# The down product of a decoder layer: copies in its first block, and the residual rows loaded in pieces in later blocks

## The chip, the cores and the metric

The kernel runs on one core of one Trainium2 chip. The metric is the device time of one execution in microseconds (us), of which the median over several executions counts. A core has five engines that matter here: TensorE (PE in the profile; its weight loads are PEld), VectorE (DVE), ScalarE (ACT), GpSimd (POOL) and SyncE (SP), which issues most of the transfers (DMAs). Each engine works through its own list of instructions in order; semaphores hold an instruction until what it reads is there and what it overwrites is no longer needed. The operands lie in an on-chip memory (SBUF, 128 partitions); PE writes its results to banks of another (PSUM).

## The reference

One layer of a decoder with three token mixers, a merge and an MLP, in float32, on 1024 tokens of width 1024. The change touches the last line only: the residual `x` plus the down product of the MLP, whose inner width is 4096.

```python
x = x + jnp.sum(gate * y, axis=2) @ w_out[layer]

h = rms_norm(x, norm_mlp[layer])
x = x + jnp.square(jax.nn.relu(h @ w_up[layer])) @ w_down[layer]
```

## The kernel before, in words

`tail` computes these lines. It first makes the residual rows `x + ... @ w_out` and stores them to DRAM as `xd`, eight tiles of 128 rows by 1024 columns. Then come the up product and the down product.

*Seven products.* Both matrix products are made by a scheme of Strassen's kind: two by two blocks are multiplied with 7 block products in place of 8, from sums of blocks on each side. The products are named by the numbers 1 to 7. On the weight side of the down product `BSIDE` says which operand each takes: products 1, 2 and 3 take the raw blocks 11, 21 and 22 of `w_down`; 6, 7, 5 and 4 take the sums t2, t3, t1 and t4, which `sums` makes on POOL when they are first asked for (L1266): t1 = 12 - 11, t2 = 22 - t1, t3 = 22 - 12, t4 = 21 - t2. So the operand of product 6 needs three raw blocks and two sums in a row.

*Splits.* Each float32 operand is split into a high and a low part (`split`): ACT copies the source into `wh`, rounded (L90), and DVE or POOL subtracts to get `wl` (L91). The pair is called a form. A product of two forms takes three matmuls (`mm3`, L119 to L121: high by high, high by low, low by high).

*The up product* runs over 16 pairs `p` of weight row blocks. The results of a pair (squares of the relu, L1431 and L1432) are turned into the seven left operands of the down product, each 128 by 512, and stored to DRAM as `ud[p][i]`.

*The down product* is the loop `for b in range(0, H, G)` with H = 16 and G = 2: eight blocks of two pairs each, here called blocks 1 to 8 (block 1 is b = 0). In each block the products come in the order 1, 6, 2, 7, 5, 4, 3. A product takes two forms per pair, one from `ud` (a load by SP at L1523, then a split on ACT and DVE) and one from `w_down` (loads by SP at L1372, sums and splits on POOL, high parts on ACT), four forms in all, and has 24 matmuls of 128 by 512: 4 groups of 128 rows, 2 pairs, 3 matmuls. A block has 168 matmuls. Products 2, 7 and 3 are accumulated into the PSUM banks of 1, 6 and 5.

*What happens to a finished bank.* Products 1, 6 and 7 go to sums `a10` to `a73` in SBUF: in block 1 ACT copies them there (L1540), later DVE adds to them (L1495). Products 2, 5, 4 and 3 belong to one half of an output tile `x1[t]` each, and DVE adds them to it (L1495). In block 1 the eight tiles `x1[t]` are loaded whole from `xd` (L1528) while the forms of products 1 and 6 are made, after the last raw block asked for until then. In block 8 the sums are put together with the tiles and the results are stored.

*Buffers.* Forms: 11, in two pools. Raw blocks `wr`: 3 in the pool `pre` and 4 in `main`. Temporaries by tag: `u` 12, `v` 4, `s` 5 and `e` 4 buffers (`HEAD` = 4). The `s` buffers hold sums of the up weights, the `e` buffers the copy of product 1 in the up product. A buffer is given out anew when the work on its last content is over, so a form of the down product can only be made when an earlier form has been used up by PE.

*Order.* PE's list follows the order of the code. The lists of DVE, ACT, POOL and SP are made when the program is built, by a planner that simulates the engines and puts each instruction where it expects it to be ready; the forms of a product thus move ahead of the matmuls as far as buffers allow, and those of block 1 stand among the last pairs of the up product.

Of the kernel before, what the change touches and what calls it, by code (L numbers as in the profile page):

```python
# [11 lines left out]
F32 = mybir.dt.float32  # L12
F32R = mybir.dt.float32r
AF = mybir.ActivationFunctionType
# [3 lines left out]
P = 128  # L18
S = 1024
D = 1024  # L20
NT = S // P
# [54 lines left out]
class Kernel:  # L76
# [1196 lines left out]
    def tail(self, mp, mh, ml, halves, pre):  # L1273
        tc, nc, a = self.tc, self.nc, self.a
        kw = dict(bufs=1, reuse_waits="tile")
        H = FF // P // 2
        xd = self.dram.tile([NT, P, D], F32, name="xd")
# [7 lines left out]
        for k in range(KT):  # L1285
            r = xp.tile([P, D], F32, name="x1", tag="x1", bufs=2)
# [50 lines left out]
        last = {}  # L1337
        HEAD = 4
        late = []
        for t in (0, 4, 1, 5, 2, 3, 6, 7):  # L1340
            ts = slice(t * P, t * P + P)
            x1 = xp.tile([P, D], F32, name="x1", tag="x1", bufs=2)
            nc.scalar.dma_start(x1, a["x"][ts, :])
            for s in halves:
                ps = self.mm()
# [14 lines left out]
        main = more = None  # L1360
        count = dict(f=0, r=0)
# [3 lines left out]
            pool, bufs = (pre, 3) if main is None or count["f"] % 11 < 3 else (main, 8)  # L1365
            return [pool.tile([P, 512], F32R, name=f"w{x}", tag=f"w{x}", bufs=bufs) for x in "hl"]

        def raw(src):
            count["r"] += 1
            pool, bufs = (pre, 3) if main is None or count["r"] % 7 < 3 else (main, 4)  # L1370
            r = pool.tile([P, 512], F32, name="wr", tag="wr", bufs=bufs)
            last["raw"] = nc.sync.dma_start(r, src).ins  # L1372
            return r

        def temp(tag="u"):
            pool, bufs = dict(u=(more, 12), v=(more, 4), s=(main, 5), e=(main, HEAD))[tag]
            return pool.tile([P, 512], F32, name=tag, tag=tag, bufs=bufs)

        def splitted(src, eng):
            f = form()  # L1380
            self.split(*f, src, eng)
            return f
# [4 lines left out]
        def up_pair(p):  # L1387
            o = Pair()
            wu = lambda n: raw(a["wu"][p + H * (n[0] == "2"), :, (int(n[1]) - 1) * 512:int(n[1]) * 512])
            get = self.sums(wu, lambda: temp("s"), "s", nc.vector)  # L1390
            o.ps, o.p4 = {}, None
# [63 lines left out]
        main = tc.alloc_tile_pool(name="main", side="right", **kw)  # L1455
# [35 lines left out]
        x1 = [acc.tile([P, D], F32, name=f"x1{t}") for t in range(NT)]  # L1491
# [3 lines left out]
        add = lambda o, x: nc.vector.tensor_tensor(o, o, x, op=ALU.add)  # L1495
        G = 2
        order = (1, 6, 2, 7, 5, 4, 3)
        banks = 0

        def bank():  # L1500
            nonlocal banks
            banks += 1
            return self.mm() if (banks - 1) % 8 < 6 else self.tr()

        for b in range(0, H, G):
            gets = []
            for p in range(b, b + G):
                wd = lambda n, p=p: raw(a["wd"][p + H * (n[0] == "2"), :, (int(n[1]) - 1) * 512:int(n[1]) * 512])
                gets.append(self.sums(wd, temp, "t", nc.gpsimd))
            held = {}  # L1510
            final = b + G == H
            if final:
                for j in range(4):
                    add(sums[6][j], sums[1][j])
                    add(x1[j][:, hi], sums[6][j])
                    add(sums[7][j], sums[1][j])
                    add(x1[4 + j][:, lo], sums[7][j])
                    add(x1[4 + j][:, hi], sums[7][j])
            for i in order:
                forms = []  # L1520
                for q in range(G):
                    u = temp("u" if b else "v")
                    nc.sync.dma_start(u, ud[b + q][i])  # L1523
                    forms.append((splitted(u, nc.vector), splitted(gets[q](self.BSIDE[i]), nc.gpsimd)))
                if b == 0 and i in (1, 6):
                    with tc.issue_after(last["raw"]):
                        for t in range(4 * (i == 6), 4 + 4 * (i == 6)):
                            nc.sync.dma_start(x1[t], xd[t])  # L1528
                chain = {2: 1, 7: 6, 3: 5}.get(i)
                if not chain:  # L1530
                    held[i] = [bank() for _ in range(4)]
                for j in range(4):
                    ps = held[chain or i][j]
                    js = slice(j * P, j * P + P)
                    for q in range(G):
                        (uh, ul), (wh, wl) = forms[q]
                        self.mm3(ps, uh[:, js], ul[:, js], wh, wl, q == 0 and not chain, q == G - 1, bool(chain))
                    if i in sums and not final:
                        if b == 0:
                            nc.scalar.activation(sums[i][j], ps, AF.Copy)  # L1540
                        else:
                            add(sums[i][j], ps)
                        continue

                    t, s = place[i](j)
                    for t, s in {1: ((j, hi), (4 + j, lo), (4 + j, hi)), 6: ((j, hi),),
                                 7: ((4 + j, lo), (4 + j, hi))}.get(i, ((t, s),)):
                        add(x1[t][:, s], ps)
                    if final and i in (2, 3, 4, 5):
                        nc.sync.dma_start(a["out"][t * P:(t + 1) * P, s], x1[t][:, s])  # L1550
# [62 lines left out]
```

## Time and profile before

| | us |
|---|---|
| three runs | 2003.59, 2010.27, 2010.7 |
| their median | 2010.27 |
| the profiled execution | 2011.07 |
| its span, first to last instruction | 2009.3 |
| what lies around the span | 1.77 |

The profile shows one execution. The mean clock that TensorE was granted in it is 0.983 of full speed. The down product begins at 1673.5 us of the span and ends with it.

A row of the timeline has the start, the duration, the engine, the line, the operation, the tile written and the tiles read, the shapes and how many instructions the row joins; in square brackets stands how long the engine was idle ahead of it and what it waited for. A row of a window has, for each engine, its busy time with the number of instructions, then TensorE's granted clock, the busy share of the DMA engines and what they moved. A row of a group has the busy time, the mean duration in ns of one instruction, and the idle time ahead of them with its releaser.

### The profile page before, as it was taken

The numbers are of one execution on the slowest core, as the hardware profiler recorded it, in microseconds if no ns is written. First come the engines' busy times: TensorE is split into PE (matmuls) and PEld (weight loads), VectorE is DVE, ScalarE is ACT, GpSimd is POOL, SyncE is SP. The second block draws the span as 40 slices with busy tenths as digits, with TensorE's granted clock in tenths as the row PEclk, the third lists the DMA queues.
The fourth block names the chain that finished last, engine by engine and source line by source line (L and its number), as shares of the span: only waits on it lengthen the run. The fifth ranks groups of instructions, "written<-read, shape, count | busy, mean of one in ns | idle before, by whom it ended". The sixth has DMA issues, their size and how long they took to land. (4 is left out here: it accounts for less than half of the span.)

```text
span 2009.3 us, 30615 instructions
## 1 busy us (share of the span) xinstructions
PE 1889.3 (94%) x9842; PEld 1616.0 (80%) x9842; DVE 1422.2 (71%) x3216; ACT 1006.1 (50%) x2550; POOL 959.3 (48%) x1138
## 2 busy tenths in 40 slices
PE   7999999998899999999999899998999998999998
PEld 6788889887788888887888677886788886888876
DVE  6757777788667677658777847648754544889898
ACT  5356555666545555545556524225554454433431
POOL 4455445643361112262232247218454545789784
PEclk9999999999999999999999899999999998999999
DMA  6131012101201111203333366425544436445343
GB/s 222 52 106 56 9 57 54 53 16 55 83 32 57 52 52 59 78 27 101 95 123 125 127 236 208 141 85 177 192 155 146 163 136 236 142 157 163 121 147 115
DMA packets 123773, 221.59 MB, mean 110 GB/s; under 512 B 14580, under 2 KB 35604, under 8 KB 123612
## 3 DMA queue, kind: packets, MB, share of 16 engines
q1 hardware_dynamic: 122028, 213.87, 32.4%
q10 hardware_dynamic: 1584, 5.77, 0.9%
q8 instruction: 78, 1.28, 0.3%
q14 instruction: 83, 0.68, 0.1%
HBM read 158.68 MB, written 64.83 MB: 111 GB/s over the span
## 5 line engine op out<-in xcount | busy, mean ns | idle before, releaser
L91 POOL TENSOR_TENSOR wl<-wr,wh 128x512 fp32r<-128x512 f32 (+3 forms) x246 | 328.5, 1342 | 261.3 <-ACT wh L90 212.6
L90 ACT ACTIVATE wh<-wr 128x512 fp32r<-128x512 f32 (+3 forms) x258 | 150.0, 590 | 189.1 <-PE mm L120 117.2
L716 PE MATMUL sc<-st 128*128 128x256 f32 (+5 forms) x736 | 183.6, 344 | 18.3 <-ACT p L748 17.7
L90 ACT ACTIVATE ph<-tr 128x384 fp32r<-128x384 f32 (+3 forms) x280 | 138.4, 497 | 118.3 <-PE tr L764 96.3
L91 DVE TENSOR_TENSOR pl<-tr,ph 128x384 fp32r<-128x384 f32 (+3 forms) x280 | 155.5, 558 | 40.1 <-ACT ph L90 38.3
L761 POOL MEMSET ph<- 128x128 f32 x152 | 33.9, 223 | 267.8 <-PE ac L904 238.3
L119 PE MATMUL mm<-hh,wh 128*128 128x512 f32 x384 | 159.8, 416 | 0.0
L716 PEld LDWEIGHTS sc<-st 128*128 128x128 f32 x736 | 123.5, 193 | 38.5 <-ACT p L748 29.5
L120 PE MATMUL mm<-hl,wh 128*128 128x512 f32 x384 | 152.4, 397 | 0.0
L121 PE MATMUL mm<-hh,wl 128*128 128x512 f32 x384 | 152.3, 397 | 0.0
L119 PE MATMUL mm<-wh 128*128 128x512 f32 x352 | 140.0, 398 | 8.4 <-DVE x L1495 5.4
L120 PE MATMUL mm<-wl,wh 128*128 128x512 f32 x352 | 139.4, 396 | 9.0 <-POOL wl L91 9.0
L90 ACT ACTIVATE wh<-u 128x512 fp32r<-128x512 f32 x162 | 93.1, 620 | 105.9 <-PE mm L120 27.8
L121 PE MATMUL mm<-wh,wl 128*128 128x512 f32 x352 | 139.0, 395 | 0.0
L764 PE MATMUL tr<-ident,p 128*128 128x128 f32 x792 | 129.8, 277 | 8.5 <-DVE st L569 7.0
L748 ACT ACTIVATE p<-sc,mc 128x256 f32<-128x256 f32 (+5 forms) x200 | 106.7, 539 | 50.8 <-DVE mc L740 47.5
L904 PE MATMUL ac<-ph,st 128*128 128x256 f32 x392 | 110.2, 299 | 18.3 <-DVE ob L911 12.3
L91 POOL TENSOR_TENSOR wl<-s,wh 128x512 fp32r<-128x512 f32 x64 | 89.2, 1401 | 77.9 <-ACT wh L90 77.9
L91 DVE TENSOR_TENSOR wl<-u,wh 128x512 fp32r<-128x512 f32 x98 | 113.6, 1160 | 4.7 <-ACT wh L90 4.7
L119 PE MATMUL mm<-wh,hh 128*128 128x384 f32 (+1 forms) x320 | 115.9, 362 | 0.6 <-ACT raw L525 0.6
L905 PE MATMUL ac<-pl,st 128*128 128x256 f32 x392 | 106.2, 291 | 7.6 <-DVE pl L91 7.0
L120 PE MATMUL mm<-wl,hh 128*128 128x384 f32 (+1 forms) x320 | 109.2, 341 | 0.0
(312 smaller groups left out, 5726.7 us busy)
## 6 DMA issues: line engine op xcount, KB each, us to landing
ud<-u SPq DMA_DIRECT2D x112, 256.0 KB, 2.1
u<-ud SPq DMA_DIRECT2D x98, 256.0 KB, 3.5
wr<-wu SPq DMA_DIRECT2D x76, 256.0 KB, 2.8
wr<-wd SPq DMA_DIRECT2D x64, 256.0 KB, 3.0
gd<-go SPq DMA_DIRECT2D x48, 256.0 KB, 2.0
g<-gd SPq DMA_DIRECT2D x48, 256.0 KB, 3.2
wr<-wg SPq DMA_DIRECT2D x40, 256.0 KB, 2.6
wr<-wbr SPq DMA_DIRECT2D x40, 256.0 KB, 3.0
```

What stands on the lines that cost most here:

```text
L90: nc.scalar.activation(hi, src, AF.Copy)
L91: (eng or nc.vector).tensor_tensor(lo, src, hi.bitcast(F32), op=ALU.subtract)
L119: mm(out, lh, rh, start=first, stop=False, skip_group_check=more)
L120: mm(out, lh, rl, start=False, stop=False, skip_group_check=more)
L121: mm(out, ll, rh, start=False, stop=last, skip_group_check=more)
L716: self.nc.tensor.matmul(ps[:, off:off + k1 - k0], q[:, t * P:(t + 1) * P], k[:, k0:k1], start=i == 0, stop=i == 1)
L748: self.last_exp = self.nc.scalar.activation(p, ps, AF.Exp, bias=m, scale=-1.0, accum_out=l).ins
L761: nc.gpsimd.memset(ph[0:rows, o:o + P].bitcast(F32), 0.0)
L764: nc.tensor.transpose(pt[0:rows, o:o + P], src, self.ident)
L904: nc.tensor.matmul(ac, v, ph, start=first, stop=False)
L905: nc.tensor.matmul(ac, v, pl, start=False, stop=last)
```

## The change

The diff touches `tail` alone.

```diff
--- before.py
+++ after.py
@@ -1365,10 +1365,13 @@
             pool, bufs = (pre, 3) if main is None or count["f"] % 11 < 3 else (main, 8)
             return [pool.tile([P, 512], F32R, name=f"w{x}", tag=f"w{x}", bufs=bufs) for x in "hl"]
 
-        def raw(src):
-            count["r"] += 1
-            pool, bufs = (pre, 3) if main is None or count["r"] % 7 < 3 else (main, 4)
-            r = pool.tile([P, 512], F32, name="wr", tag="wr", bufs=bufs)
+        def raw(src, spare=False):
+            if spare:
+                r = main.tile([P, 512], F32, name="wr", tag="e", bufs=HEAD)
+            else:
+                count["r"] += 1
+                pool, bufs = (pre, 3) if main is None or count["r"] % 7 < 3 else (main, 4)
+                r = pool.tile([P, 512], F32, name="wr", tag="wr", bufs=bufs)
             last["raw"] = nc.sync.dma_start(r, src).ins
             return r
 
@@ -1495,6 +1498,8 @@
         add = lambda o, x: nc.vector.tensor_tensor(o, o, x, op=ALU.add)
         G = 2
         order = (1, 6, 2, 7, 5, 4, 3)
+        rest = [(t, s) for t in range(NT) for s in halves]
+        count["x"] = 0
         banks = 0
 
         def bank():
@@ -1505,8 +1510,9 @@
         for b in range(0, H, G):
             gets = []
             for p in range(b, b + G):
-                wd = lambda n, p=p: raw(a["wd"][p + H * (n[0] == "2"), :, (int(n[1]) - 1) * 512:int(n[1]) * 512])
-                gets.append(self.sums(wd, temp, "t", nc.gpsimd))
+                wd = lambda n, p=p: raw(a["wd"][p + H * (n[0] == "2"), :, (int(n[1]) - 1) * 512:int(n[1]) * 512], p == 1)
+                early = iter("ss" if b == 0 else "")
+                gets.append(self.sums(wd, lambda early=early: temp(next(early, "u")), "t", nc.gpsimd))
             held = {}
             final = b + G == H
             if final:
@@ -1522,10 +1528,12 @@
                     u = temp("u" if b else "v")
                     nc.sync.dma_start(u, ud[b + q][i])
                     forms.append((splitted(u, nc.vector), splitted(gets[q](self.BSIDE[i]), nc.gpsimd)))
-                if b == 0 and i in (1, 6):
-                    with tc.issue_after(last["raw"]):
-                        for t in range(4 * (i == 6), 4 + 4 * (i == 6)):
-                            nc.sync.dma_start(x1[t], xd[t])
+                if b and rest and count["x"] % 2 == 0:
+                    t, s = rest.pop(0)
+                    r = main.tile([P, 512], F32, name="xr", tag="e", bufs=HEAD)
+                    nc.sync.dma_start(r, xd[t][:, s])
+                    add(x1[t][:, s], r)
+                count["x"] += 1
                 chain = {2: 1, 7: 6, 3: 5}.get(i)
                 if not chain:
                     held[i] = [bank() for _ in range(4)]
@@ -1543,6 +1551,9 @@
                         continue
 
                     t, s = place[i](j)
+                    if b == 0:
+                        nc.scalar.activation(x1[t][:, s], ps, AF.Copy)
+                        continue
                     for t, s in {1: ((j, hi), (4 + j, lo), (4 + j, hi)), 6: ((j, hi),),
                                  7: ((4 + j, lo), (4 + j, hi))}.get(i, ((t, s),)):
                         add(x1[t][:, s], ps)
```

In block 1 nothing is loaded into `x1[t]` any more: products 2, 5, 4 and 3 of that block are copied there by ACT, as products 1, 6 and 7 are copied to their sums. The residual comes later: from block 2 on, at every second product, as long as any of 16 pieces is left, a piece of `xd` (128 rows by 512 columns) is loaded into a buffer of the tag `e`, as `xr`, and added to its half of `x1[t]` by DVE with both inputs in SBUF.

The second part concerns buffers in block 1. Its first two sums of each pair, t1 and t2, are made in buffers of the tag `s` instead of `u`. The raw blocks of its second pair (p = 1) go to buffers of the tag `e` and no longer count in the rotation of the `wr` buffers.

The planner's lists move as follows. Lines behind the change have other numbers in the changed program: L1495 becomes L1498, L1540 becomes L1548, L1431 and L1432 become L1434 and L1435.

**POOL, from the end of the up product into block 1.** Before: `wr_18918` and `wr_18930` are block 11 of the two pairs, 18978 and 18996 block 22, 18980 and 18998 block 12, 19050 and 19062 block 21. The sums into `u_18982` and `u_18984` are t1 and t2 of the first pair, `u_19000` and `u_19002` those of the second.

```order
L91 TENSOR_TENSOR wl_18921<-wr_18918,wh_18920 128x512
L91 TENSOR_TENSOR wl_18933<-wr_18930,wh_18932 128x512
L91 TENSOR_TENSOR wl_19053<-wr_19050,wh_19052 128x512
L1266 TENSOR_TENSOR u_18982<-wr_18980,wr_18918 128x512
L1266 TENSOR_TENSOR u_18984<-wr_18978,u_18982 128x512
L1266 TENSOR_TENSOR u_19000<-wr_18998,wr_18930 128x512
L91 TENSOR_TENSOR wl_18987<-u_18984,wh_18986 128x512
L1266 TENSOR_TENSOR u_19002<-wr_18996,u_19000 128x512
L1266 TENSOR_TENSOR u_19102<-wr_18978,wr_18980 128x512
L1266 TENSOR_TENSOR u_19114<-wr_18996,wr_18998 128x512
L1266 TENSOR_TENSOR u_19206<-wr_19050,u_18984 128x512
L91 TENSOR_TENSOR wl_19005<-u_19002,wh_19004 128x512
```

After: 18974 and 18992 are block 22, 18976 and 18994 block 12. The row of `s_18980` is t2 of the first pair (its t1 stands three rows ahead of it); the `wl` rows from 18767 to 18853 are splits of the last up pair.

```order
L1266 TENSOR_TENSOR s_18980<-wr_18974,s_18978 128x512
L91 TENSOR_TENSOR wl_18767<-s_18743,wh_18766 128x512
L91 TENSOR_TENSOR wl_18786<-wr_18783,wh_18785 128x512
L91 TENSOR_TENSOR wl_18807<-s_18804,wh_18806 128x512
L91 TENSOR_TENSOR wl_18830<-wr_18741,wh_18829 128x512
L91 TENSOR_TENSOR wl_18853<-s_18850,wh_18852 128x512
L91 TENSOR_TENSOR wl_18921<-wr_18918,wh_18920 128x512
L91 TENSOR_TENSOR wl_18933<-wr_18930,wh_18932 128x512
L91 TENSOR_TENSOR wl_18983<-s_18980,wh_18982 128x512
L1266 TENSOR_TENSOR s_18996<-wr_18994,wr_18930 128x512
L1266 TENSOR_TENSOR s_18998<-wr_18992,s_18996 128x512
L91 TENSOR_TENSOR wl_19001<-s_18998,wh_19000 128x512
```

Both sums of the first pair now stand ahead of five splits of the last up pair, and those of the second pair directly behind the split of the first pair's t2. The split of block 21 of the first pair (`wl_19053` before, `wl_19045` after), an operand of product 2, stood ahead of all these sums and now stands behind them, and the t3 and t4 sums (`u_19102`, `u_19114`, `u_19206` before) no longer stand between the two t2 splits.

**ACT at the same place.** Before, the copies of product 1 into `a10` to `a13` stand ahead of the high parts of both t2 operands, `wh_18986` and `wh_19004`.

```order
L1431 ACTIVATE u_18869<-u_18764 128x512
L1540 ACTIVATE a10_18900<-mm_18940 128x512
L1432 ACTIVATE u_18869<-u_18869 128x512
L1540 ACTIVATE a11_18901<-mm_18941 128x512
L1540 ACTIVATE a12_18902<-mm_18942 128x512
L1540 ACTIVATE a13_18903<-mm_18943 128x512
L90 ACTIVATE wh_18986<-u_18984 128x512
L90 ACTIVATE wh_18992<-v_18990 128x512
L90 ACTIVATE wh_19004<-u_19002 128x512
```

After, these high parts are `wh_18982` and `wh_19000`; `u_18801` is a result of the last up pair.

```order
L90 ACTIVATE wh_18932<-wr_18930 128x512
L90 ACTIVATE wh_18970<-v_18968 128x512
L90 ACTIVATE wh_18982<-s_18980 128x512
L90 ACTIVATE wh_18988<-v_18986 128x512
L1434 ACTIVATE u_18801<-mm_18724 128x512
L1435 ACTIVATE u_18801<-u_18801 128x512
L90 ACTIVATE wh_19000<-s_18998 128x512
L90 ACTIVATE wh_19038<-v_19036 128x512
```

Both now stand among the last up pair's work, and the first copy of product 1 follows eight rows behind `wh_19038`.

**DVE in block 2, product 2.** `x10` to `x13` are output tiles, `mm_` banks of PSUM, the `wl_` rows splits of `u` operands. Before:

```order
L91 TENSOR_TENSOR wl_19535<-u_19532,wh_19534 128x512
L1495 TENSOR_TENSOR x10_18892<-x10_18892,mm_19328 128x512
L91 TENSOR_TENSOR wl_19545<-u_19542,wh_19544 128x512
L1495 TENSOR_TENSOR x11_18893<-x11_18893,mm_19329 128x512
L1495 TENSOR_TENSOR x12_18894<-x12_18894,mm_19330 128x512
L1495 TENSOR_TENSOR x13_18895<-x13_18895,mm_19331 128x512
L91 TENSOR_TENSOR wl_19587<-u_19584,wh_19586 128x512
L1495 TENSOR_TENSOR a70_18908<-a70_18908,mm_19396 128x512
L91 TENSOR_TENSOR wl_19599<-u_19596,wh_19598 128x512
```

After, with the pieces `xr_19606` and `xr_19840`:

```order
L91 TENSOR_TENSOR wl_19533<-u_19530,wh_19532 128x512
L1498 TENSOR_TENSOR x10_18892<-x10_18892,mm_19320 128x512
L91 TENSOR_TENSOR wl_19543<-u_19540,wh_19542 128x512
L1498 TENSOR_TENSOR x11_18893<-x11_18893,mm_19321 128x512
L1498 TENSOR_TENSOR x11_18893<-x11_18893,xr_19606 128x512
L1498 TENSOR_TENSOR x12_18894<-x12_18894,mm_19322 128x512
L1498 TENSOR_TENSOR x12_18894<-x12_18894,xr_19840 128x512
L1498 TENSOR_TENSOR x13_18895<-x13_18895,mm_19323 128x512
L91 TENSOR_TENSOR wl_19585<-u_19582,wh_19584 128x512
L1498 TENSOR_TENSOR a70_18908<-a70_18908,mm_19391 128x512
L91 TENSOR_TENSOR wl_19597<-u_19594,wh_19596 128x512
```

The list is the same but for two adds of pieces among those from PSUM. All sixteen stand in this way among adds from PSUM and splits: two at the end of block 1, then 4, 3, 4 and 3 in blocks 2 to 5, the two shown among them. From block 6 on DVE's list differs in one exchanged pair of rows.

On SP the loads of whole `x1[t]` tiles stood among the last stores of `ud`, seven of them between the stores of products 2 and 5 of the last pair, ahead of five loads of `w_down`. After, the first `xr` load stands between the stores of products 1 and 4 of the last pair, and the others are spread among the loads of `u` and `w_down` of the blocks that follow.

## Prediction

> **What bounds the kernel now.** I read the span and the engines' shares first, then cut the down product into stretches.
>
> ```profile
> span 2009.3 us, 30615 instructions
> PE 1889.3 (94%) x9842; PEld 1616.0 (80%) x9842; DVE 1422.2 (71%) x3216; ACT 1006.1 (50%) x2550; POOL 959.3 (48%) x1138
> core 0: us, PE busy (x) PEld busy (x) DVE busy (x) ACT busy (x) POOL busy (x), PEclk, DMA share, GB/s
> 1673.50:1678.90 5.40, 5.40 (x25) 4.32 (x23) 4.95 (x5) 3.58 (x6) 3.57 (x3) 1.00 0.88 309
> 1678.90:1694.10 15.20, 8.12 (x20) 5.42 (x20) 3.85 (x5) 5.53 (x10) 10.91 (x9) 0.66 1.03 390
> 1700.00:1912.00 212.00, 211.37 (x932) 174.71 (x931) 181.84 (x228) 87.71 (x159) 176.65 (x120) 1.00 0.44 143
> 1912.00:1982.20 70.20, 60.53 (x245) 46.63 (x243) 68.36 (x84) 22.82 (x41) 54.64 (x35) 0.95 0.37 118
> 1982.20:2006.30 24.10, 23.40 (x102) 19.05 (x102) 21.62 (x33) 5.02 (x9) 7.88 (x5) 1.00 0.43 160
> ```
>
> TensorE (PE) bounds the program, and the down product has three regimes. From 1700 to 1912 PE is busy for 211.4 of 212 us. From 1912 to 1982 VectorE (DVE) is, 68.4 of 70.2 us, and PE does only 245 matmuls. And in 1678.9 to 1694.1, inside block 1, nothing is full but the DMA engines: PE is busy for 8.1 of 15.2 us. That hole is what the change can reach. PE's rows in it:
>
> ```profile
> 1673.50 0.39 PE L119 MATMUL mm<-wh 128*128 128x512 f32 x1
> 1678.71 0.39 PE L121 MATMUL mm<-wh,wl 128*128 128x512 f32 x1
> 1680.31 0.50 PE L119 MATMUL mm<-wh 128*128 128x512 f32 x1 [1.20 <-ACT wh L90]
> 1681.65 0.50 PE L120 MATMUL mm<-wl,wh 128*128 128x512 f32 x1 [0.84 <-POOL wl L91]
> 1683.99 0.79 PE L119 MATMUL mm<-wh 128*128 128x512 f32 x1 [1.60 <-ACT wh L90]
> 1688.21 0.79 PE L120 MATMUL mm<-wl,wh 128*128 128x512 f32 x1 [3.43 <-POOL wl L91]
> 1688.81 0.63 PE L121 MATMUL mm<-wh,wl 128*128 128x512 f32 x1
> 1693.50 0.53 PE L120 MATMUL tr<-wl,wh 128*128 128x512 f32 x1
> 1693.87 0.39 PE L121 MATMUL tr<-wh,wl 128*128 128x512 f32 x1
> ```
>
> Product 1 of block 1 has 24 matmuls, started in 1673.50 to 1678.71: 5.21/23 = 0.2265 us each, 5.44 per product, 38.05 per block. Product 6 should begin at 1678.94. Full pace returns with the start at 1693.87, 14.93 us later, and 17 matmuls were done by then (five from 1680.31 to 1688.21, twelve from 1688.81 to 1693.50), which need 17 x 0.2265 = 3.85. **The hole costs 14.93 - 3.85 = 11.08 us.** Of it 2.4 is clock: the last twelve came 4.69/11 = 0.426 apart, 0.20 too slow.
>
> ```profile
> 1682.00:1684.00 2.00, 0.40 (x3) 0.01 (x1) 0.15 (x1) 0.63 (x1) 2.00 (x2) 0.89 1.03 334
> 1684.00:1686.00 2.00, 0.78 (x1) 0.27 (x1) 0.00 (x0) 0.00 (x0) 2.00 (x3) 0.50 0.95 337
> ```
>
> The granted clock fell to 0.50 after gaps of 1.4, 1.1 and 1.8 us with single matmuls between them. The Trainium skill, "TensorE: Matmul & The Clock Gate", section "Part 1: The HAM clock gate", says half clock follows an idle window of about 3.4 us, free-running; by it gaps like these need not lower the clock, and the hole would be 8.7; here they did, so the measured 11.08 stands.
>
> What ends last in the hole is on POOL and ScalarE (ACT):
>
> ```profile
> 1671.51 1.30 POOL L91 TENSOR_TENSOR wl<-wr,wh 128x512 fp32r<-128x512 f32 x1 [15.01 <-ACT wh L90]
> 1672.77 1.30 POOL L1266 TENSOR_TENSOR u<-wr 128x512 f32<-128x512 f32 x1
> 1681.56 1.71 POOL L1266 TENSOR_TENSOR u<-wr,u 128x512 f32<-128x512 f32 x1
> 1683.24 2.48 POOL L1266 TENSOR_TENSOR u<-wr 128x512 f32<-128x512 f32 x2
> 1685.68 1.25 POOL L1266 TENSOR_TENSOR u<-wr,u 128x512 f32<-128x512 f32 x1
> 1686.90 1.25 POOL L91 TENSOR_TENSOR wl<-u,wh 128x512 fp32r<-128x512 f32 x1
> 1679.14 0.60 ACT L1540 ACTIVATE a<-mm 128x512 f32<-128x512 f32 x1 [0.76 <-PE mm L121]
> 1679.63 0.62 ACT L90 ACTIVATE wh<-u 128x512 fp32r<-128x512 f32 x1
> 1683.30 0.63 ACT L90 ACTIVATE wh<-u 128x512 fp32r<-128x512 f32 x1 [2.53 <-POOL u L1266]
> ```
>
> POOL stood 15 us before a split meant for product 2, so the sums for product 6 began only at 1672.77; the first `wh` of it then waited on ACT behind four copies of product 1 (the last at 1679.14), and the second half's `wl` (1686.90) behind three sums that nobody needed yet. It is an order, and the saturated DMA is not its cause.
>
> **The change, part by part.**
>
> *Earlier sums and reordering (gain 11.08).* The changed program makes `t1`, `t2` of pair 0 among the forms of the last up pair, where POOL has 1.3 us splits 2.7 us apart or more, and those of pair 1 right after the split of pair 0's `t2`; no split of product 2 stands before any of them now. On ACT both `wh` stand ahead of the first copy. I date them by the old rows: the form buffers come free with the up products (5.44/2 = 2.72 us each, the last ending at 1673.5), so pair 0's `t2` can be split near 1660, pair 1's by about 1669, ten microseconds before 1678.94. New sum rows on POOL are 1.3 each and lie in its idle 15 us. What is late next would be the product 2 split of pair 1: its buffer frees with product 1 near 1678.3, it takes ACT 0.62 and POOL 1.3 to 1.75, and it is needed after 1684.4. So I take the whole 11.08; the bounds are 9.7 (the 1.4 us gap stays) and 11.08.
>
> *Residual loads moved.* Eight loads of 512 KB, 8.3 us each to landing, leave block 1; 16 of 256 KB come in blocks 2 to 5, the same 4 MB over 152 us: 27 GB/s on top of 143, no bound. SP issues them in its one order: 16 issues against 8, 0.38 us each as in the row below, and from the fifth on each waits for a buffer that an earlier add frees.
>
> ```profile
> 1761.61 0.38 SPq L1523 DMA_DIRECT2D u<-ud  x1
> ```
>
> *Sixteen adds of block 1 become ACT copies.* The DVE add from PSUM was 0.679; the ACT copy is 0.60 and ACT is busy for 87.7 of 212 us. Hidden under PE; DVE has 10.9 us less in block 1.
>
> *Sixteen adds come to DVE, 2 at the end of block 1, 4, 3, 4 and 3 in blocks 2 to 5.* Both inputs lie in SBUF, and before has no such add beside a PE at full pace. The nearest rows:
>
> ```profile
> L91 DVE TENSOR_TENSOR wl<-u,wh 128x512 fp32r<-128x512 f32 x73 | 85.9, 1178 | 2.4 <-ACT wh L90 2.4
> L91 DVE TENSOR_TENSOR wl<-v,wh 128x512 fp32r<-128x512 f32 x4 | 5.9, 1503 | 1.8 <-ACT wh L90 1.8
> L1495 DVE TENSOR_TENSOR x<-x,mm 128x512 f32<-128x512 f32 x79 | 53.3, 679 | 11.7 <-PE mm L121 11.2
> L1495 DVE TENSOR_TENSOR x<-x,a x12: 678/918/1801, 1949.8 to 1973.0; 128x512 f32<-128x512 f32 x12
> 1658.65 0.68 DVE L91 TENSOR_TENSOR wl<-v,wh 128x512 fp32r<-128x512 f32 x1
> x<-xd SPq DMA_DIRECT2D x8, 512.0 KB, 8.3
> ```
>
> An add costs from 0.68 (POOL idle, as in the row at 1658.65) to 1.80; I take 1.18, the mean of the 73 splits that also read two SBUF tiles in that very stretch. DVE idles 212 - 181.84 = 30.2 us there, 5.4 per block and 21.7 in blocks 2 to 5. Fourteen adds take 16.5 (9.5 to 25.2). At 1.18 they fit, also in a block with four (4.7 of 5.4). Cover of a late add: its PSUM bank is wanted soonest after product 3, 0.75 product or 4.1 us later. At 1.80 they overrun by 3.5 us, to which a half-clock stretch of 2.4 may come: 5.9. Cost taken: 0.
>
> *The end.* From 1912 DVE holds PE, as its 68.4 of 70.2 us show. From block 6 on its order is the same but for one swapped pair, so the 24 + 70 us move as a whole, if DVE comes there without a backlog; block 6 has no added add and 5.4 us of idle to clear one.
>
> **Sum.** The profiled run took 2011.07 (2009.3 span and 1.77 around it). 2011.07 - 11.08 + 0 = **2000.0**. That execution is 0.8 over the median 2010.27 and near the highest of the three (2003.59 to 2010.7); I don't correct for it. About 0.5% is what a measurement of this kernel can tell from no change: 2000.2 from the median, which happens to lie on my number.
>
> **Rivals.**
>
> *DVE and POOL crowd each other in blocks 2 to 5.* For it: splits cost 1.18 instead of 0.68 beside POOL. Against: 21.7 us of idle. Price 5.9 at the upper bound: 2005.9. Were the two never at work at the same time, POOL's 120 instructions at the lone 1.30 and DVE's 73 + 4 splits at 0.68 would hold 208.4 of the 212 us already, and 2.6 of the free 3.6 would fall to blocks 2 to 5; fourteen adds more, 9.5 us, overrun that by 6.9: 2006.9. The Trainium skill, "SBUF — State Buffer", section "Who interferes with whom", states this: a DVE instruction with two SBUF inputs and a GpSimd one that reads SBUF exclude each other for the whole instruction; the trace agrees in kind (0.68 alone, 1.18 beside POOL).
>
> *The hole shrinks but stays.* A gap of 1.4 at 1678.94 remains: 2001.4; with a half-clock stretch 2003.8. For it: the lists on ACT and POOL are long and in order. Against: ten microseconds of lead.
>
> *The end gains too.* POOL's order in the last block differs:
>
> ```profile
> 1959.63 0.50 PE L120 MATMUL mm<-wl,wh 128*128 128x512 f32 x1 [2.76 <-POOL wl L91]
> ```
>
> If this 2.76 goes and DVE profits: 1997.2. Against: DVE was busy all through it.
>
> *Slower than before: SP's queue.* A residual load waits for a DVE add, and behind it stand the `u` and `wd` loads of the next products. From issue to a form a load needs 0.38 + 3.5 + 0.62 + 1.18 = 5.7 us. Eleven form buffers at four a product let the splits run 1.75 products, 9.5 us, ahead of PE. If DVE lags by over 9.5 - 5.7 = 3.8 us the loads come late, PE stops as in the hole, and DVE lags more. Two such holes: 2000.0 + 22.2 = 2022. Against: a lag of that size is cleared within a block by the 5.4 us of idle, and a wait for SP stops none of the work that already lies loaded.
>
> ```profile
> u<-ud SPq DMA_DIRECT2D x98, 256.0 KB, 3.5
> ```
>
> That the residual isn't moved out of block 1 is excluded: the changed order has no load of it before the last up stores and no PSUM add in block 1.
>
> **How the numbers follow.** Forecast 2000.0 (1998 to 2002): 0.52. DVE and POOL crowd: 0.20. Hole stays in part: 0.12. The end gains: 0.12. SP's queue: 0.04. The range for 8 in 10 reaches from 1995.5 (1997.2 less half a microsecond of spread and 1.2 for a clock stretch in the end saved) to 2007.5 (2006.9 and half a microsecond of spread); SP's queue is left out. Faster by over 0.5% is under 2000.2: 0.36 of the forecast's 0.52, as the median lies 0.8 under the profiled run, and the end's 0.12: 0.48. Within 0.5%: 0.16 + 0.20 + 0.12 = 0.48. Slower: 0.04.
>
> **What would show it.** PE's rows around 1679 run on at 0.23 us with the granted clock at 1.00, and POOL's two `t2` sums lie before that. DMA share in block 1 falls from 1.03 to under 0.7. In blocks 2 to 5 DVE is busy for over 93%, the new adds have a mean near 1.2, and PE has no gap over 0.5 us; a gap there with DVE or POOL as releaser speaks for the first rival, one with a DMA as releaser for SP's queue. From block 7 on DVE is full as before, with PE's last 102 matmuls unbroken. The forecast is wrong if a stall outside 1679 to 1694 changes by over 2 us.

## The result, and the profile after

| | before | after |
|---|---|---|
| median of six runs (us) | 2009.19 | 1996.87 |
| lowest and highest | 2003.59, 2014.93 | 1993.05, 2003.03 |
| profiled execution | 2011.07 | 1996.93 |
| its span | 2009.3 | 1995.1 |

The ratio of after to before is 0.9948, 95% interval 0.9933 to 0.9963: faster by 0.5%, 10.4 us, between 7.4 and 13.5. The two medians alone lie 12.3 us apart, within that interval.

First the totals of the changed kernel, with the same columns as before.

```profile
span 1995.1 us, 30648 instructions
PE 1883.6 (94%) x9842; PEld 1612.9 (81%) x9842; DVE 1432.7 (72%) x3216; ACT 1013.8 (51%) x2566; POOL 966.1 (48%) x1138
```

The down product has 1344 matmuls, 168 to a block, and the trace of each kernel has them all, so the stretches can be cut exactly where a block starts: block 1, blocks 2 to 6, blocks 7 and 8. The windows of before:

```profile
1673.50:1722.67 49.17, 42.09 (x169) 33.39 (x168) 31.25 (x34) 23.92 (x44) 37.69 (x27) 0.90 0.69 247
1722.67:1914.04 191.37, 190.74 (x841) 157.63 (x840) 164.32 (x208) 77.17 (x140) 161.30 (x109) 1.00 0.45 148
1914.04:2005.44 91.40, 81.73 (x337) 63.99 (x335) 88.82 (x115) 26.78 (x49) 60.47 (x39) 0.96 0.37 123
```

and of after:

```profile
1670.18:1708.26 38.08, 38.08 (x170) 31.53 (x168) 27.97 (x20) 29.64 (x56) 32.66 (x21) 1.00 0.58 197
1708.26:1900.73 192.47, 191.00 (x841) 157.53 (x840) 178.15 (x223) 77.59 (x142) 165.48 (x109) 1.00 0.50 163
1900.73:1991.39 90.66, 82.78 (x337) 65.40 (x335) 86.48 (x112) 26.77 (x48) 60.86 (x39) 0.92 0.37 123
```

Block 1 became **11.09 us** shorter and PE is now busy in all of it. Blocks 2 to 6 became 1.10 longer, blocks 7 and 8 0.74 shorter. That is 10.73 us less for the down product (331.94 before, 321.21 after, with the last matmul). The span is some 14 us shorter; of the rest 3.32 lies ahead of the down product, which began at 1673.50 before and at 1670.18 after, and some 0.1 behind it.

The first two rows, of PE's timeline, are the end of product 1 and the start of product 6 in block 1; POOL's and ACT's rows show when the operands of product 6 were made. Again from the profile of the changed kernel:

```profile
1675.39 0.39 PE L121 MATMUL mm<-wh,wl 128*128 128x512 f32 x1
1675.62 0.39 PE L119 MATMUL mm<-wh 128*128 128x512 f32 x1
1656.29 1.29 POOL L91 TENSOR_TENSOR wl<-s,wh 128x512 fp32r<-128x512 f32 x1 [0.16 <-ACT wh L90]
1661.43 1.29 POOL L1266 TENSOR_TENSOR s<-wr 128x512 f32<-128x512 f32 x1 [3.86 <-DMA wr<-wd]
1662.80 1.29 POOL L1266 TENSOR_TENSOR s<-wr,s 128x512 f32<-128x512 f32 x1
1664.83 1.29 POOL L91 TENSOR_TENSOR wl<-s,wh 128x512 fp32r<-128x512 f32 x1 [0.74 <-ACT wh L90]
1664.12 0.63 ACT L90 ACTIVATE wh<-s 128x512 fp32r<-128x512 f32 x1 [1.68 <-POOL s L1266]
1671.74 0.60 ACT L1548 ACTIVATE a<-mm 128x512 f32<-128x512 f32 x1
```

Product 6 follows product 1 by 0.23 us. Its two t2 splits (the rows that read `s`) began at 1656.29 and 1664.83, 19.3 and 10.8 us ahead of it, and ACT made the second high part 7.6 us before its first copy of product 1.

### The profile page after: what moved, and what is told of

Its sections match the earlier page's. It is cut to its first block, busy times and chain, and to the rows that moved or that the text cites. A ratio compares the mean times of both kernels' runs of the same rounds, so it can differ in the third digit from the quotient of the medians.

```text
span 1995.1 us, 30648 instructions
## 1 busy us (share of the span) xinstructions
PE 1883.6 (94%) x9842; PEld 1612.9 (81%) x9842; DVE 1432.7 (72%) x3216; ACT 1013.8 (51%) x2566; POOL 966.1 (48%) x1138
## 5 line engine op out<-in xcount | busy, mean ns | idle before, releaser
L91 POOL TENSOR_TENSOR wl<-wr,wh 128x512 fp32r<-128x512 f32 (+3 forms) x246 | 329.2, 1344 | 255.8 <-ACT wh L90 208.6
L91 POOL TENSOR_TENSOR wl<-s,wh 128x512 fp32r<-128x512 f32 x68 | 95.1, 1406 | 78.6 <-ACT wh L90 78.5
L904 PE MATMUL ac<-ph,st 128*128 128x256 f32 x392 | 110.2, 299 | 17.8 <-DVE ob L911 11.9
```

The lines of the kernel that those rows point to most:

```text
L91: (eng or nc.vector).tensor_tensor(lo, src, hi.bitcast(F32), op=ALU.subtract)
L904: nc.tensor.matmul(ac, v, ph, start=first, stop=False)
```

## The experiments

All kernels below are cut in the same way. The numbers are us from the first to the last matmul of each stretch; the down product's start is that of its first matmul in the span.

```
kernel                        start    block 1  2 to 6   7 and 8  span
before                        1673.50  49.17    191.37   91.40    2009.3
after                         1670.18  38.08    192.47   90.66    1995.1
after, once more              1670.29  38.08    192.54   90.58    1995.2
sums part alone               1672.79  38.08    191.57   90.55    1996.7
residual part alone           1666.46  50.46    192.74   91.81    2006.4
tag s alone                   1664.49  38.08    191.54   92.33    1990.2
spare raw buffers alone       1669.76  50.70    191.54   90.53    2006.3
tag s, first pair             1671.25  45.48    191.46   93.37    2005.4
tag s, second pair            1672.08  45.36    191.54   91.84    2004.6
after, no pieces              1667.35  38.08    191.55   90.84    1991.6
after, pieces added twice     1664.16  38.08    196.75   92.13    1994.9
sums, block 8 folded, POOL    1670.00  38.08    191.57   92.77    1996.3
sums, folded, POOL last       1667.06  38.08    191.30   85.86    1989.3
sums, folded, DVE only        1668.04  38.08    191.54   89.27    1991.6
```

### The changed kernel once more

No edit.

> The changed kernel once more, for the spread of one profile: block 1 38.1, blocks 2 to 6 within 0.5 us of 192.5, blocks 7 and 8 within 0.5 us of 90.7; the start of the down product may move by several us, as it lay between 1664.5 and 1673.5 us in six kernels whose program ahead of the last up pairs is the same.

It took 1997.02 us. The blocks came out within 0.08 us of the first profile. In this one repeat the stages of a kernel thus come out within a tenth of a us, and differences of 0.9 us between kernels can be read there. What does not repeat between kernels is the start of the down product: it lies between 1664.16 and 1673.50 in the fourteen profiles, and before happens to be the latest of all. This spread is there long before the change can act: PE's 8001st matmul starts between 1550.39 and 1560.62 us, again latest before, while the lists of PE, DVE, ACT and POOL are the same in all fourteen up to some 50 us ahead of the down product.

### One part of the change at a time

The sums part alone: the pieces' loop goes out, the loads of whole tiles and the adds of block 1 come back.

```diff
-                if b and rest and count["x"] % 2 == 0:
...
-                    add(x1[t][:, s], r)
-                count["x"] += 1
+                if b == 0 and i in (1, 6):
+                    with tc.issue_after(last["raw"]):
+                        for t in range(4 * (i == 6), 4 + 4 * (i == 6)):
+                            nc.sync.dma_start(x1[t], xd[t])
...
-                    if b == 0:
-                        nc.scalar.activation(x1[t][:, s], ps, AF.Copy)
-                        continue
```

> The changed kernel with its early sums and spare raw buffers alone: the whole x1 tiles are loaded in block 1 and added to there by DVE, as before. Order theory: the hole of block 1 comes from POOL's and ACT's order, so block 1 takes 38.1 us as in the changed kernel (49.2 before) although DMA is as full as before; the time is that of the changed kernel or some 2 us less, as the sixteen adds of pieces are gone. DMA theory (the 4 MB of residual loads in block 1 made the operands late): block 1 takes 44 us or more.

The residual part alone: the changed kernel with these two lines.

```diff
-                ..., p == 1)
-                early = iter("ss" if b == 0 else "")
+                ...)
+                early = iter("")
```

> The changed kernel with its residual part alone (copies in block 1, pieces loaded and added in later blocks); sums t1 and t2 of block 1 and all raw blocks in the buffers of before. POOL's order puts both t2 sums behind the splits of the up product again. Order theory: block 1 takes 45 to 49 us, and the time is that of before within 5 us. DMA theory: block 1 takes 40 us or less and the time is near the changed kernel's.

The sums part alone ran in 1998.49 us (median of 4), ratio to before 0.9947 (0.9930 to 0.9965): the whole gain. The residual part alone ran in 2010.66 (10 runs), ratio 1.0004 (0.9989 to 1.0020): none of it. Windows over the first two products of block 1, at full pace 10.9 us long; the columns are those of the other windows, the last two the DMA share and GB/s. Before, then the sums part alone, then the residual part alone:

```profile
1673.50:1695.47 21.97, 14.89 (x49) 10.86 (x48) 9.24 (x9) 10.29 (x19) 15.86 (x12) 0.77 1.00 369
```

```profile
1672.79:1683.66 10.87, 10.87 (x49) 9.01 (x48) 9.42 (x8) 8.36 (x16) 10.24 (x7) 1.00 0.98 356
```

```profile
1666.46:1689.72 23.26, 14.06 (x49) 10.26 (x48) 9.95 (x9) 10.27 (x19) 18.52 (x14) 0.78 0.66 215
```

With the whole tiles still being loaded and the DMA engines 0.98 full, PE runs without a gap; with the DMA share down to 0.66 the hole is as wide as ever. The DMA theory falls, the order theory stands. Block 1 of the residual part alone took 50.46 us, a little above the 45 to 49 expected and 1.3 above before: PE's last wait for POOL in the hole is 5.55 us there and was 3.43.

### Which part of the sums part

The kernel with the sums part alone, without the spare raw buffers, and then without the tag s:

```diff
-                ..., p == 1)
+                ...)
```

> As the kernel with the sums part alone, but the raw blocks of the second pair of block 1 stay in the rotation of before; only t1 and t2 go to the tag s. POOL's order has the sums of the first pair early and those of the second pair where they can be ready a few rows later. If the tag s alone does it: block 1 within 1 us of 38.1. If the spare raw buffers are needed too, for block 12 and 22 of the second pair: 40 to 46 us.

```diff
-                early = iter("ss" if b == 0 else "")
+                early = iter("")
```

> As the kernel with the sums part alone, but t1 and t2 stay in the tag u; only the raw blocks of the second pair go to the tag e. POOL's order keeps the sums behind the last splits of the up product. Order theory: block 1 takes 45 to 49 us as before, since the u buffers and not the raw blocks held the sums back. If the raw blocks were what came late: 38 to 41 us.

They took 1992.07 and 2008.06 us (one run each). Block 1 is 38.08 with the tag s alone, and 50.70 with the spare raw buffers alone. POOL's rows of the latter show that the raw blocks were not what came late:

```profile
1667.77 1.30 POOL L91 TENSOR_TENSOR wl<-wr,wh 128x512 fp32r<-128x512 f32 x1 [11.03 <-ACT wh L90]
1669.02 1.31 POOL L1266 TENSOR_TENSOR u<-wr 128x512 f32<-128x512 f32 x1
```

POOL stands 11 us before a split as it stood 15 before the change, and the first sum follows right behind, with no wait of its own. (The 50.70 is above the 45 to 49 expected, for the same longer wait for POOL, 5.83 us.) What the spare buffers do is elsewhere: blocks 7 and 8 take 90.53 with them and 91.40 without (before); 90.55 with them and 92.33 without where the tag s is in.

The kernel with the tag s alone, narrowed to one pair, so that it differs from the kernel before in two sums:

```diff
-                early = iter("ss" if b == 0 else "")
+                early = iter("ss" if p == 0 else "")
```

> The kernel before with one edit: t1 and t2 of the first pair of block 1 go to the tag s, those of the second pair stay in u. If both pairs are needed (the hole is two stalls, the second one for the second pair's low part): the first stall goes, the second stays in part, block 1 takes 41 to 46 us, its first low-part wait shows on POOL. If the first pair alone made the hole: within 1 us of 38.1.

and with `p == 1`:

> The kernel before with one edit: t1 and t2 of the second pair go to the tag s, those of the first pair stay in u. The first pair's operand is needed first and its sums stay behind the last splits of the up product, so the first stall stays; block 1 takes 41 to 46 us. If the hole is one queue that only has to be shortened by two sums anywhere, 39 us or less.

They took 2007.10 and 2006.37 us (one run each); block 1 is 45.48 and 45.36, so either pair alone leaves two thirds of the hole (7.4 and 7.3 of 11.1 us). PE's longest waits in it, with the rows of POOL behind the longer one, for the first pair early and then for the second pair early:

```profile
1678.05 0.50 PE L119 MATMUL mm<-wh 128*128 128x512 f32 x1 [0.53 <-ACT wh L90]
1682.28 0.79 PE L120 MATMUL mm<-wl,wh 128*128 128x512 f32 x1 [3.72 <-POOL wl L91]
1673.14 3.44 POOL L1266 TENSOR_TENSOR u<-wr 128x512 f32<-128x512 f32 x2
1680.51 1.71 POOL L91 TENSOR_TENSOR wl<-u,wh 128x512 fp32r<-128x512 f32 x1
```

```profile
1678.89 0.49 PE L119 MATMUL mm<-wh 128*128 128x512 f32 x1 [1.21 <-ACT wh L90]
1683.10 0.79 PE L120 MATMUL mm<-wl,wh 128*128 128x512 f32 x1 [3.71 <-POOL wl L91]
1673.98 3.44 POOL L1266 TENSOR_TENSOR u<-wr 128x512 f32<-128x512 f32 x2
1681.34 1.71 POOL L91 TENSOR_TENSOR wl<-u,wh 128x512 fp32r<-128x512 f32 x1
```

It is the same wait for whichever pair's sums are late, behind the same queue on POOL: the late pair's t2 is done by 1673.2 and 1674.0, and its split stands behind the sums t3 and t4 of both pairs, which products 7 and 4 want later. Only with both pairs early is the queue no longer in the way. These waits are 4.3 and 4.9 us of the two holes; most of the rest is clock, as the matmuls right behind them start 0.4 us apart and more, where 0.23 is full pace.

### The price of the pieces

The changed kernel without the pieces, and with every piece added twice:

```diff
-                if b and rest and count["x"] % 2 == 0:
...
-                count["x"] += 1
```

> The changed kernel without loads and adds of the pieces (so the residual is left out). If the pieces are what delays POOL's split by 1.5 us ahead of block 5, blocks 2 to 6 take 190.4 to 191 us (192.5 in the changed kernel, 190.4 is PE's own pace). If POOL's order alone does it, the delay stays as in the kernel with the sums part alone: 191.6. Block 1 as in the changed kernel, 38.1.

```diff
                     add(x1[t][:, s], r)
+                    add(x1[t][:, s], r)
```

> The changed kernel with every piece of the residual added twice (so the residual counts double). Theory of idle time: an add of 1.1 us goes into DVE's idle time until that is used up; blocks 2 to 5 have about 11 us of it left in the changed kernel and get 14 adds more, 15.6 us, so blocks 2 to 6 take 194 to 198 us (192.5 with single adds). Theory of exclusion (DVE with two SBUF inputs and POOL never at work together): POOL and DVE are full at the single adds already and each further add costs its 1.1 us in full: 205 us or more. If the pieces are free: below 193.

They took 1993.65 and 1996.93 us (one run each). Blocks 2 to 6 are 191.55, 192.47 and 196.75 with none, single and double adds. So the wait for POOL's split at the start of block 5 is not made by the pieces, as the first guess had it (190.4 to 191): the 1.15 above PE's pace that the kernel without them has is the same wait that the sums part alone has. The pieces make it longer. The windows of none and double (the single one stands above), and the groups of adds of pieces, first in the double and then in the single case:

```profile
1705.43:1896.98 191.55, 190.70 (x842) 157.63 (x840) 164.89 (x209) 77.59 (x142) 161.58 (x109) 1.00 0.46 149
```

```profile
1702.24:1898.99 196.75, 191.32 (x841) 157.46 (x840) 193.51 (x238) 77.49 (x142) 168.24 (x109) 1.00 0.50 160
L1498 DVE TENSOR_TENSOR x<-x,xr 128x512 f32<-128x512 f32 x29 | 37.5, 1303 | 0.2
```

```profile
L1498 DVE TENSOR_TENSOR x<-x,xr 128x512 f32<-128x512 f32 x14 | 15.6, 1117 | 0.3
```

Fourteen adds keep DVE busy for 13.3 us more and cost PE 0.92; fifteen further ones take 15.4 more and cost 4.28, and then DVE is busy for 193.5 of 196.75 us. The time is in the range of the theory of idle time (194 to 198) and far from that of exclusion. But PE's longest waits with double adds show that DVE's idle time is only a part of it:

```profile
1786.38 0.50 PE L120 MATMUL mm<-wl,wh 128*128 128x512 f32 x1 [1.47 <-POOL wl L91]
1821.64 0.50 PE L120 MATMUL mm<-wl,wh 128*128 128x512 f32 x1 [2.30 <-POOL wl L91]
1864.86 0.50 PE L119 MATMUL mm<-wh 128*128 128x512 f32 x1 [1.65 <-DVE x L1498]
```

One of the three is for DVE itself; the other two, the larger part, are for splits on POOL, as with single adds.

The way in which the single adds cost most of their 0.92 us shows in the rows around the start of block 5. POOL and then PE in the kernel without pieces, its lines left out where POOL works on:

```profile
1809.63 1.80 POOL L1266 TENSOR_TENSOR u<-wr,u 128x512 f32<-128x512 f32 x1 [3.21 <-issue]
...
1820.28 1.26 POOL L91 TENSOR_TENSOR wl<-wr,wh 128x512 fp32r<-128x512 f32 x1
...
1821.59 0.50 PE L120 MATMUL mm<-wl,wh 128*128 128x512 f32 x1 [0.85 <-POOL wl L91]
```

and in the changed kernel:

```profile
1812.51 1.30 POOL L1266 TENSOR_TENSOR u<-wr,u 128x512 f32<-128x512 f32 x1 [2.86 <-DMA wr<-wd]
...
1818.89 1.74 POOL L1266 TENSOR_TENSOR u<-wr,u 128x512 f32<-128x512 f32 x1
1820.59 3.45 POOL L1266 TENSOR_TENSOR u<-wr 128x512 f32<-128x512 f32 x2
1824.00 1.27 POOL L91 TENSOR_TENSOR wl<-wr,wh 128x512 fp32r<-128x512 f32 x1
1825.32 0.50 PE L120 MATMUL mm<-wl,wh 128*128 128x512 f32 x1 [1.47 <-POOL wl L91]
```

In both, POOL's last idle time ends at the same moment, 10.0 us ahead of the block's start at full pace (1819.67 and 1822.50), and from there it works without a break until the split is done: 11.9 us without pieces, 12.8 with them, at up to 1.8 us an instruction that takes 1.27 alone. The eight instructions are the same in both. Its busy time in blocks 2 to 6 goes from 161.58 to 165.48. So the adds are not late themselves; beside them POOL is slower, its split comes later, and PE waits for it 1.47 us, against 0.85. That is 0.6 of the 0.92; the rest is mostly in shorter waits in block 4, which were not followed.

The Trainium skill, "SBUF — State Buffer", section "Who interferes with whom", has it that a DVE instruction with two SBUF inputs contends with a GpSimd instruction that reads SBUF, that the ports which the two engines share are an exclusive lock, and that whoever issues first gets them for the whole instruction. An estimate by these sentences taken together, from lone durations in the traces (1.28 for POOL's 109 instructions, 0.68 for DVE's 70 splits and 29 adds), gives 206.8 us for the doubled adds, 10 more than were measured. POOL's instructions beside DVE's come 1.73 us apart where the two durations make 1.96, so in these runs the two engines do hold each other up, but not for all of the instruction.

### A version that goes further

Blocks 7 and 8 cost 90.7 us where PE needs 76.2, and PE's waits there name DVE. So the sums part alone was taken and block 8 written anew: product 1 is added once to its sums, and the sums are put together during block 8 instead of ahead of it. First with twelve of those adds on POOL:

```diff
-            if final:
-                for j in range(4):
...
+                    if final and i == 1:
+                        add(sums[1][j], ps)
+                        padd(sums[6][j], sums[1][j])
+                        add(sums[7][j], sums[1][j])
+                        continue
...
+                    if final and i == 6:
+                        add(x1[4 + j][:, lo], sums[7][j])
+                        padd(x1[4 + j][:, hi], sums[7][j])
+                    if final and i == 2:
+                        padd(x1[j][:, hi], sums[6][j])
```

> The kernel with the sums part alone, with block 8 written anew: product 1 is added to its sums once (4 adds from PSUM where there were 12) ahead of the sums' own adds, and 12 of those 20 adds go to POOL, which is half idle in block 8. If DVE bounds blocks 7 and 8 (24 adds fewer of about 0.7 to 1.2 us each), they take 80 to 85 us in place of 90.6, and the time is 1988 to 1993. If POOL's adds hold POOL's splits of block 8 back, they take 88 us or more.

It took 1998.41 us (median of 4), ratio to before 0.9951 (0.9932 to 0.9971), and blocks 7 and 8 took 92.77 (DVE's adds are 20 fewer by the code, not 24). The rival of that expectation came true, as PE's longest wait and POOL's rows ahead of it show:

```profile
1964.03 4.68 POOL L1499 TENSOR_TENSOR x<-x,a 128x512 f32<-128x512 f32 x3
1968.67 1.26 POOL L91 TENSOR_TENSOR wl<-u,wh 128x512 fp32r<-128x512 f32 x1
1969.98 0.79 PE L120 MATMUL mm<-wl,wh 128*128 128x512 f32 x1 [6.98 <-POOL wl L91]
```

Three adds that could wait stand ahead of the split that PE waits for: the fault of block 1 over again.

Then with four adds on POOL only, put behind its last split, and sixteen on DVE; and with all on DVE, at the places of the first attempt. The first of the two:

```diff
+                if final and i == 3:
+                    with tc.issue_after(self.last_split):
+                        for j in range(4):
+                            nc.gpsimd.tensor_tensor(x1[j][:, hi], x1[j][:, hi], sums[6][j], op=ALU.add)
...
+                    if final and i == 6:
+                        add(sums[7][j], sums[1][j])
+                    if final and i == 2:
+                        add(sums[6][j], sums[1][j])
+                    if final and i == 7:
+                        add(x1[4 + j][:, hi], sums[7][j])
+                        add(x1[4 + j][:, lo], sums[7][j])
```

> The kernel with the sums part alone, block 8 written anew as before, but with only the four adds that are wanted last (those of product 6's sums) on POOL, behind POOL's last split; the other sixteen stay on DVE, spread over products 1 to 7 of block 8. In the first attempt product 1 of block 8 took 5.4 us in place of 14 once DVE was relieved, and POOL's adds then held splits back by 4.4 and 7.0 us. If that was the whole of the loss: blocks 7 and 8 take 77 to 81 us, the time is 1983 to 1990. If DVE's 44 adds of block 8 then end late instead: the last product ends on time and the tail behind PE's last matmul grows from 4 to some 10 us: 1990 to 1995.

> The same with all adds on DVE and those of the sums at products 1, 6 and 2 of block 8. Eight adds from PSUM fewer than in the kernel with the sums part alone, 5.4 us; if DVE bounds the end, blocks 7 and 8 take 84 to 87 us in place of 90.6; if only the place of the adds matters, within 1 us of 90.6 or above.

The first took 1993.20 us (median of 4), ratio to before 0.9936 (0.9915 to 0.9958); the one with all adds on DVE 1994.63 (one run). With POOL's adds last, blocks 7 and 8 take 85.86 us and not the 77 to 81 that were expected; the time is in the range of the other guess, 1990 to 1995:

```profile
1896.44:1982.30 85.86, 79.38 (x337) 61.98 (x335) 78.21 (x99) 26.66 (x48) 64.22 (x43) 1.00 0.35 117
```

DVE, with 48 adds in block 8 by the code where 44 were counted, is still the fullest engine beside PE there. Its adds hold PE up in the last products and not only behind them, and the tail behind PE's last matmul grew from 3.7 to 7.0 us, so of 4.8 us saved against the changed kernel 1.5 remain here; with 1.2 in blocks 2 to 6 it is 2.7 us less from the start of the down product to the end (322.2 against 324.9). In whole runs the intervals of the two kernels overlap, so the profile shows the gain and the times do not yet. With all adds on DVE the stretch takes 89.27: above the 84 to 87 of one guess and just below the 89.6 of the other, so that run decides between neither.

## Where the prediction was right and where it was not, point by point

*The hole of block 1* (11.08 us forecast, 11.09 measured). Cause, size and its end were right: the stalls were POOL's and ACT's order, and that the DMA engines were full there had no part in it. The dates were close too: the t2 splits were expected 19 and 10 us ahead of product 6 and came 19.3 and 10.8 ahead. What the prediction did not tell apart is which edit does it. The tag s alone does; the spare raw buffers have no part in it. One reading is a little off: the clock did not wait for all three gaps, as its mean is 0.54 already from 1683.50 to 1684.00 before, and the third gap ended at 1683.99. The 2.4 us of clock stay as they are.

*What is late next.* Nothing is, in block 1: PE is busy in all of its 38.08 us, and the low part for product 2 that was named came in time.

*Residual loads and copies.* Priced at nothing, and they are: moving the loads out of block 1 gave nothing, and block 1 runs at full pace with 56 instructions on ACT against 44.

*The sixteen adds.* The duration was near (1.12 measured, 1.18 taken). The cost was taken as 0 and is 0.92 us, so **the term of the sum that was mis-sized is this one**. The cover was sought in DVE's idle time, which did suffice; the cost came through POOL, which each add slows. It is the first rival, at a sixth of its price of 5.9. DVE was busy for 92.4% of blocks 2 to 5 (forecast: over 93%), and the gap of 1.47 us with POOL as its releaser is over the 0.5 that was named as the limit. 0.85 of that gap is there without the pieces too.

*The end.* Taken as unmoved; it became 0.74 us shorter. The rival expected 2.8, if the wait of 2.76 for POOL in block 8 went and DVE profited. That wait did go. PE's longest waits in block 8 of the changed kernel are all for DVE:

```profile
1942.24 0.62 PE L119 MATMUL mm<-wh 128*128 128x512 f32 x1 [1.84 <-DVE x L1498]
1951.32 0.80 PE L119 MATMUL mm<-wh 128*128 128x512 f32 x1 [2.87 <-DVE x L1498]
1968.13 0.50 PE L119 MATMUL mm<-wh 128*128 128x512 f32 x1 [2.06 <-DVE x L1498]
```

So the rival's condition came and most of its gain did not, for the reason that the prediction gave against it: DVE was busy all through. By the letter this also meets the prediction's own sign of being wrong, a stall outside 1679 to 1694 that changes by over 2 us, although the stretch around it changed by less. The runs tie it to the spare raw buffers: in the five kernels without them (before, the residual part alone, the tag s alone, the two with one pair early) PE waits 2.3 to 2.8 us for POOL at that place. In those that have them and the block 8 of before it does not, and in the two pairs of kernels that differ in these buffers alone blocks 7 and 8 take 0.9 and 1.8 us less with them. That the rotation of the raw blocks is what moves POOL there was not tested.

*SP's queue.* PE's waits in blocks 2 to 6 name no load; POOL's wait for one there (2.86 us ahead of 1812.51) ended as late without the pieces.

*The sum.* 2000.0 forecast; the profiled run took 1996.93, the median is 1996.87: inside the range for 8 in 10 (1995.5 to 2007.5), outside the 1998 to 2002 of the forecast itself. It lies next to the 1997.2 of the rival that the end gains too, and that is chance, since the end gave 0.74. The down product's own balance is -11.09 + 1.10 - 0.74 = -10.73, close to the 11.08 taken. The remaining 3.3 us, which took the time 1.1 below the forecast's own 1998 to 2002, is the base: the sum was made against an execution in which everything ahead of the down product took longest among fourteen. That part is the same in all these kernels but for its last 50 us, and the spread is there before them: at the 8001st matmul the kernel before is 4.36 us later than the changed one. So it is a spread of single runs and nothing that the change does. The prediction saw that its base was near the highest of three runs and did not correct for it. It gave faster and unchanged by 0.5% the same chance, 0.48; the ratio of 0.9948 fell just on the faster side.

## What to carry to other kernels

When PE stops while the DMA engines are full, look first at what each waiting engine's queue holds: here the sums of product 6 stood behind a split that was wanted later, and a transfer of 4 MB beside them cost nothing. Which buffer a short-lived operand is taken from decides how early it can be placed in that queue; four sums made in the buffers of another tag gave the whole gain, while the larger part of the change gave nothing and cost 0.9 us. An added instruction that fits into its own engine's idle time can still cost, through an engine that it slows, so both are to be counted.

## What the runs showed of the hardware

A DVE instruction with two inputs in SBUF and a POOL instruction beside it stretch each other. DVE's 0.68 us alone became 1.12 (the adds) and 1.18 (the splits) in the mean, POOL's 1.27 became 1.73 where DVE's stood beside it for most of its time. That is 0.46 us for POOL, less than the DVE instruction's own time, and near the most that a pair costs: over blocks 2 to 6, POOL's busy time grew by 3.90 us for fourteen adds and by 2.76 for fifteen more, 0.28 and 0.18 each.

The stages of the down product came out within 0.1 us in two executions of the changed kernel, while the start of that product moved by 9.3 us among fourteen profiles whose program up to shortly before it is the same. A gain of 0.5% in whole runs therefore needs many of them, and in the stage it belongs to it can be read from one.
